# Retention by (scores · h) · w_v in place of scores · (h · w_v), with a new order of the heads' work

## The chip, the cores and the metric

The kernel runs on one core of a Trainium2 chip (trn2). The metric is the device time of one launch in microseconds (us), as the median of the runs shown. All weights come from HBM in each launch, through queues that five engines share: TensorE (PE) multiplies, ScalarE (ACT) and VectorE (DVE) prepare operands and empty PSUM, GpSimd (POOL) does a little elementwise work, SyncE (SP) issues nearly all transfers.

## What is computed

Two transformer blocks run on 256 tokens of width 1024. The part that changes is the retention of the second block. A context `ctx` of 256 tokens and the sequence `x` are normed and modulated to `hc` and `h` (1024 features each), and both give keys and values; the sequence gives queries. With the two directions and both chunk states multiplied out, what four heads (queries and keys of 256, values of 512 features) do is

```
k, v   = rows of [hc; h] @ w_k, [hc; h] @ w_v      # 512 keys; rope on the sequence's q and k
scores = (q @ k.T) / 16 * decay                    # 256 queries x 512 keys, fixed decay by distance
o      = scores @ v                                # 256 x 512 per head
on     = (o - mean) / sqrt(var + eps)              # group norm of a head's 512 values
r     += (silu(h @ w_g) * on * gn_w) @ p_ret       # summed over the heads
y      = (sigmoid(h @ w_ga) * r + sigmoid(h @ w_gf) * fourier) @ w_out
```

The sum over features of `h @ w_v` and the sum over keys of `scores @ v` can be taken in either order.

## The kernel before, in words

Every fp32 product is made of three matmuls: `mm3` (L113) multiplies high and low parts (`wh`/`hh`, `wl`/`hl`), and `split` (L104, L105) makes such a pair, the high part by a cast on ACT and the low part by a subtraction on DVE. A weight is a block of 128x1024 (512 KB): SP loads it into one of four `raw` buffers, and `split` fills one of three pairs `wh`, `wl`. So seven blocks can be ahead of TensorE. `lin` (L129) multiplies two blocks with all 256 tokens into one PSUM tile `mm`: 48 matmuls of 256 columns. `lin_tok` (L142) takes four blocks and gives a result with tokens as rows: two tiles, 48 matmuls of 512 columns. `acc_rows` (L238) adds a block's rows into four PSUM tiles that stay open (24 matmuls of 256 columns). PSUM has eight banks: two `mm`, two `at`, four `acc`.

The order on each engine is that of a scheduler which fills TensorE from whatever is ready, by the order of the program. It is fixed when the program is built, and each engine then works its list in order.

The places that the change touches, in the order of time:

- **Fourier stage.** Per group, `dft_d` and `dft_l` are two products with ACT and DVE work in between, then `four` adds into `fo`. A list `side` gives TensorE something between them: `gf` (gates, 48 matmuls), `ctx_k` (the context's keys of a head, 48) and `ctx_v` (the context's values of a head, 48 of 512 columns). Keys and values of the context go to DRAM (`kc_d`, `vc_d`), since SBUF is full.
- **Retention stage**, four heads. `ret_vg` makes the sequence's values (48 of 512 columns) and splits them into `vh`, `vl`, reads the context's values back (`vcr`) and splits them too, and makes the gate `sg` (96 of 256 columns). `ret_kq` makes key and query with rope (96 of 256) and reads the context's keys back (`kcr`). `ret_att` makes the scores `rs` (24 of 256) and multiplies them with the values into `ro` (24 of 512), then norms (`on`). `ret_rows` turns `on` (8 transposes `rt`), multiplies by gate and gain into `fz`, splits it (`zh`, `zl`), and adds four blocks of `p_ret` into `ra` (96 of 256).
- The order of heads is written by hand at the end: `ret_att(hd)`, `ret_vg(hd + 1)`, `ret_rows(hd)`, `ret_kq(hd + 1)`. In the last head the gate `sga` (eight blocks) stands where the next head's values would.

Of the kernel before, what the change touches and what calls it, by code (L numbers as in the profile page):

```python
# [11 lines left out]
FT = mybir.dt.float32  # L12
FR = mybir.dt.float32r
# [3 lines left out]
AF = mybir.ActivationFunctionType  # L17
# [8 lines left out]
PAD = 96  # L26
# [16 lines left out]
def block_kernel(ctx: ExitStack, tc: tile.TileContext, I, out):  # L43
    nc = tc.nc
    V, S, T = nc.vector, nc.scalar, nc.tensor
# [6 lines left out]
    tmp = {"gr": None, "side": 0, "first": 4, "b": 4}  # L52
# [6 lines left out]
    dram = ctx.enter_context(tc.tile_pool(name="dram", bufs=1, space=bass.MemoryType.DRAM))  # L59
# [12 lines left out]
    ident, iota, blk2 = misc[:, 0:128], misc[:, 128:256], misc[:, 256:258]  # L72
# [4 lines left out]
    def mm_tile(name="mm", tag="mm"):  # L77
        return ps.tile([128, 2, 256], FT, name=name, tag=tag)
# [35 lines left out]
    def mm3(o, lh, ll, rh, rl, start, stop, **kw):  # L114
        T.matmul(o, lh, rh, start=start, stop=False, **kw)  # L115
        T.matmul(o, lh, rl, start=False, stop=False, **kw)  # L116
        tmp["mm"] = T.matmul(o, ll, rh, start=False, stop=stop, **kw)  # L117

    def lin(srcs, rhs, sink, nk=8, eng=V):


        for j in range(0, len(srcs), 2):
            n = min(2, len(srcs) - j)
            p = mm_tile()
            for e in range(n):
# [359 lines left out]
    for n in range(2):  # L485
        p = ps.tile([128, 4, 128], FT, name="cbp", tag="mm")
# [5 lines left out]
    h = modulated(x, col("norm1_w", 0, 8), m1(1), m1(0), bc=bc1)  # L492
# [205 lines left out]
    h2 = modulated(x, col("norm2_w", 0, 8), m1(4), m1(3), gap=(mod2, 0, 3, 5))  # L698
# [125 lines left out]
    for t0 in range(0, 256, 4):  # L824
        o = wp.tile([128, 2, 4, 128], FT, name="o", tag="raw", bufs=4)
# [112 lines left out]
    V.tensor_scalar(gate, mx(2), 0.5, None, op0=OP.mult)  # L938
    cp = cst.enter_context(tc.tile_pool(name="cp", bufs=1))
    kc_d = dram.tile([4, 128, 2, 256], FT, name="kc_d")  # L940
    vc_d = dram.tile([4, 2, 128, 512], FT, name="vc_d")
    ups = ctx_ups()
    h = modulated(x, col("norm_ffn1_2", 0, 8), mx(1), mx(0), gap=(ups, 2, 12, 8))
    run(ups)
# [45 lines left out]
            nc.sync.dma_start(kc_d[hd], k)  # L990
        lin([I["w_in_2k"][2 * hd], I["w_in_2k"][2 * hd + 1]], hc, sink)

    def ctx_v(hd):
        def sink(tb, p):
            v = tmp["p"].tile([128, 512], FT, name="vcs", tag="h2")
            S.copy(v, p)
            nc.sync.dma_start(vc_d[hd, tb], v)
        lin_tok([I["w_in_2v"][hd, q] for q in range(4)], hc, sink)


    fp = cst.enter_context(tc.tile_pool(name="fp", bufs=1))
# [16 lines left out]
    def gf(j):  # L1018
        lin([I["w_in_2gf"][2 * j + i] for i in range(2)], h,
            lambda _, p: S.activation(fg[:, 2 * j:2 * j + 2], p, AF.Sigmoid))  # L1020
# [59 lines left out]
    def ret_vg(hd):  # L1080
        vh = rp2.tile([128, 4, 512], FR, name="vh", tag="vh")
        vl = rp2.tile([128, 4, 512], FR, name="vl", tag="vl")
        lin_tok([I["w_in_2v"][hd, q] for q in range(4)], h,
                lambda tb, p: split(p, vh[:, 2 + tb], vl[:, 2 + tb]))
        vcr = rp.tile([128, 2, 512], FT, name="vcr", tag="vcr")
        nc.sync.dma_start(vcr, vc_d[hd].rearrange("b p n -> p b n"))
        split(vcr, vh[:, 0:2], vl[:, 0:2])
        sg = rp2.tile([128, 4, 256], FT, name="sg", tag="sg")
        lin([I["w_in_2g"][4 * hd + i] for i in range(4)], h,
            lambda j, p: S.activation(sg[:, 2 * j:2 * j + 2], p, AF.Silu))  # L1090
        return vh, vl, sg

    def ret_kq(hd):
        kq = {}
        for nm, w in (("k", "w_in_2k"), ("q", "w_in_2q")):
            def rsink(_, p):
                ac = rp.tile([128, 2, 256], FT, name="ac", tag="ac")
                as_ = rp.tile([128, 2, 256], FT, name="as", tag="as")
                V.tensor_tensor(ac, p, cos.unsqueeze(1).to_broadcast([128, 2, 256]), op=OP.mult)
                V.tensor_tensor(as_, p, sin.unsqueeze(1).to_broadcast([128, 2, 256]), op=OP.mult)  # L1100
                r = rp.tile([128, 2, 256], FT, name="rr", tag="rr")
                V.tensor_sub(r[:, 0], ac[:, 0], as_[:, 1])
                V.tensor_add(r[:, 1], as_[:, 0], ac[:, 1])
                rh = rp.tile([128, 2, 256], FR, name=nm + "h", tag=nm + "h")
                rl = rp.tile([128, 2, 256], FR, name=nm + "l", tag=nm + "l")
                split(r, rh, rl)
                kq[nm] = (rh, rl)
            lin([I[w][2 * hd], I[w][2 * hd + 1]], h, rsink)
        kcr = rp.tile([128, 2, 256], FT, name="kcr", tag="kcr")
        nc.sync.dma_start(kcr, kc_d[hd])  # L1110
        kch = rp.tile([128, 2, 256], FR, name="kch", tag="kch")
        kcl = rp.tile([128, 2, 256], FR, name="kcl", tag="kcl")
        split(kcr, kch, kcl)
        return (kch, kcl), kq["k"], kq["q"]

    def ret_att(hd, vh, vl, kc, kx, q):
        sh = rp.tile([128, 4, 256], FR, name="sdh", tag="sdh")
        sl = rp.tile([128, 4, 256], FR, name="sdl", tag="sdl")
        for b2_, (kh, kl) in enumerate((kc, kx)):
            p = mm_tile("rs", "at")  # L1120
            for jb in range(2):
                for d in range(2):
                    m = slice(jb * 128, jb * 128 + 128)
                    mm3(p[:, jb], kh[:, d, m], kl[:, d, m], q[0][:, d], q[1][:, d], d == 0, d == 1)
            sd = rp.tile([128, 2, 256], FT, name="sd", tag="sd")
            V.scalar_tensor_tensor(sd, p, 1.0 / 16, dec[:, hd, 2 * b2_:2 * b2_ + 2], op0=OP.mult, op1=OP.mult)
            split(sd, sh[:, 2 * b2_:2 * b2_ + 2], sl[:, 2 * b2_:2 * b2_ + 2])
        on = rp.tile([128, 2, 512], FT, name="on", tag="on")
        for ib in range(2):
            t = slice(ib * 128, ib * 128 + 128)  # L1130
            p = mm_tile("ro", "at").rearrange("p a b -> p (a b)")
            for jb in range(4):
                mm3(p, sh[:, jb, t], sl[:, jb, t], vh[:, jb], vl[:, jb], jb == 0, jb == 3)
            st = rp2.tile([128, 6], FT, name="st", tag="st")
            V.bn_stats(st, p)
            mv = rp2.tile([128, 2], FT, name="mv", tag="mv")
            V.bn_aggr(mv, st)
            vv = rp2.tile([128, 1], FT, name="vv", tag="vv")
            V.tensor_scalar(vv, mv[:, 1:2], EPS, None, op0=OP.add)
            r1 = rsqrt(vv, [128, 1], "ra")  # L1140
            V.tensor_scalar(on[:, ib], p, mv[:, 0:1], r1, op0=OP.subtract, op1=OP.mult)
        return on

    def ret_rows(hd, on, sg):
# [16 lines left out]
                for e in range(2):  # L1161
                    acc_rows(acc, [rows[e]], [zs[e]], hd + c2_ + e == 0, False)

    vg, kq = ret_vg(0), ret_kq(0)
    for hd in range(4):
        on = ret_att(hd, *vg[:2], *kq)
        sg = vg[2]
        if hd < 3:
            vg = ret_vg(hd + 1)
        else:  # L1170
            lin([I["w_in_2ga"][i] for i in range(8)], h,
                lambda j, p: S.activation(sga[:, 2 * j:2 * j + 2], p, AF.Sigmoid))
# [128 lines left out]
```

## Time and profile before

| | |
|---|---|
| median of 3 runs | 2092.63 us (2092.53 to 2097.37) |
| the profiled execution: its own time | 2094.46 us |
| its span, first to last instruction | 2092.7 us |
| PE / DVE / ACT busy, share of the span | 97% / 69% / 51% |
| Fourier stage | 1460 to 1610 us of the span |
| retention stage | 1610 to 1861 us |

Matmuls are pipelined. A row of the timeline gives a matmul some 0.28 us, though the next one starts 0.113 us later, and a "busy" PE includes such overlap. What a matmul costs on TensorE is therefore taken from starts: the start of the first of a run, that of the first after it, and the count between. A gap shows as "idle before", with the releaser; it is shorter than the issue time lost, as the last matmul before it still counts as busy.

### The profile page before, as it was taken

What the parts mean: (1) busy time and instruction counts of PE and PEld (TensorE: products, weight loads), DVE (VectorE), ACT (ScalarE), POOL (GpSimd) and SP (SyncE); (2) the same over time, 40 slices, a digit from 0 to 9 for tenths busy, and PEclk for the clock granted to TensorE, in tenths of its full rate; (3) what the DMA queues carried; (4) which work ended last, traced back from release to release, by engine and by line L of the source; (5) the groups of instructions that cost most, each with busy time, mean ns of one, the idle gap of its engine ahead of it and who ended that gap; (6) DMA issues with size and microseconds to landing.
All of it is one profiled execution on the core that took longest, in us unless ns stands there. A gap on an engine that the chain in (4) does not pass through costs nothing.

```text
span 2092.7 us, 40502 instructions
## 1 busy us (share of the span) xinstructions
PE 2020.9 (97%) x16362; PEld 1932.9 (92%) x16362; DVE 1434.2 (69%) x2687; ACT 1057.8 (51%) x1754; POOL 113.9 (5%) x95
## 2 busy tenths in 40 slices
PE   6999997899999999999999999999999999999998
PEld 3987897788999999999999999999999999989998
DVE  5877989697567777777777666636644667666555
ACT  2544553598454455445555557534544444444443
POOL 1000165200000000000000000000000000010000
PEclk8999998899999999999999999999999999999998
DMA  8956644213576766767777665535456554444553
GB/s 330 332 172 233 210 162 142 80 68 134 193 244 240 250 243 242 258 240 247 244 258 254 211 218 186 202 115 163 142 191 230 183 177 151 158 137 158 194 192 111
DMA packets 115851, 413.08 MB, mean 197 GB/s; under 512 B 12880, under 2 KB 14416, under 8 KB 115152
## 3 DMA queue, kind: packets, MB, share of 16 engines
q1 hardware_dynamic: 111248, 395.29, 55.8%
q0 software_dynamic: 4128, 14.68, 2.0%
q8 instruction: 128, 2.10, 0.4%
q10 hardware_dynamic: 288, 0.52, 0.1%
q14 instruction: 59, 0.48, 0.1%
HBM read 404.15 MB, written 6.29 MB: 196 GB/s over the span
## 4 chain that ended last, share of the span: by engine, by line
PE 77%; DVE 2%; DMA 1%; issue 1%; ACT 0%; POOL 0%; DVEq 0%; SPq 0%; ACTq 0%; POOLq 0%
PE va L116 6%; PE va L117 6%; PE va L115 6%; PE ua L115 5%; PE ua L117 5%; PE ua L116 5%; PE mm L115 4%; PE mm L117 4%; PE mm L116 4%; PE fu L116 4%; PE fu L115 4%; PE fu L117 4%; PE gps L838 2%; PE fa L116 2%; PE fa L117 2%; PE fa L115 2%
## 5 line engine op out<-in xcount | busy, mean ns | idle before, releaser
L105 DVE TENSOR_TENSOR wl<-raw,wh 128x1024 fp32r<-128x1024 f32 x588 | 726.8, 1238 | 503.2 <-ACT wh L104 499.1
L104 ACT CAST wh<-raw 128x1024 fp32r<-128x1024 f32 x613 | 643.5, 1052 | 809.9 <-issue 375.7
L117 PE MATMUL ua<-hh,wl 128*128 128x256 f32 x1024 | 282.8, 276 | 1.2 <-DVE wl L105 1.2
L116 PE MATMUL va<-zl,wh 128*128 128x256 f32 x1024 | 282.3, 276 | 1.2 <-DVE zl L105 1.2
L115 PE MATMUL ua<-hh,wh 128*128 128x256 f32 x1024 | 282.8, 276 | 0.0
L115 PE MATMUL va<-zh,wh 128*128 128x256 f32 x1024 | 281.4, 276 | 1.4 <-DVE cy L464 1.4
L116 PE MATMUL ua<-hh,wh 128*128 128x256 f32 x1024 | 282.6, 276 | 0.0
L117 PE MATMUL va<-zh,wl 128*128 128x256 f32 x1024 | 282.2, 276 | 0.0
L116 PE MATMUL mm<-hh,wh 128*128 128x256 f32 x776 | 218.1, 281 | 6.1 <-DVE hh L196 6.1
L115 PE MATMUL mm<-hh,wh 128*128 128x256 f32 x776 | 217.8, 281 | 2.1 <-ACT hh L194 1.4
L117 PE MATMUL mm<-hh,wl 128*128 128x256 f32 x776 | 217.8, 281 | 0.0
L115 PE MATMUL fu<-hh,wh 128*128 128x256 f32 x704 | 195.9, 279 | 2.7 <-ACT hh L199 1.7
L116 PE MATMUL fu<-hh,wh 128*128 128x256 f32 x704 | 195.9, 278 | 0.9 <-DVE hh L200 0.9
L117 PE MATMUL fu<-hh,wl 128*128 128x256 f32 x704 | 195.6, 278 | 0.0
L116 PEld LDWEIGHTS va<-zl,wh 128*128 128x128 f32 x1024 | 192.3, 188 | 1.4 <-DVE zl L105 1.4
L117 PEld LDWEIGHTS ua<-hh,wl 128*128 128x128 f32 x1024 | 192.1, 188 | 1.6 <-DVE wl L105 1.6
L115 PEld LDWEIGHTS va<-zh,wh 128*128 128x128 f32 x1024 | 191.4, 188 | 1.6 <-DVE cy L464 1.6
L115 PEld LDWEIGHTS ua<-hh,wh 128*128 128x128 f32 x1024 | 192.4, 188 | 0.0
L117 PEld LDWEIGHTS va<-zh,wl 128*128 128x128 f32 x1024 | 192.3, 188 | 0.0
L116 PEld LDWEIGHTS ua<-hh,wh 128*128 128x128 f32 x1024 | 192.1, 188 | 0.0
L116 PEld LDWEIGHTS mm<-hh,wh 128*128 128x128 f32 x776 | 146.9, 189 | 7.3 <-DVE hh L196 6.8
L115 PEld LDWEIGHTS mm<-hh,wh 128*128 128x128 f32 x776 | 147.4, 190 | 4.5 <-ACT hh L194 1.5
(415 smaller groups left out, 4516.0 us busy)
## 6 DMA issues: line engine op xcount, KB each, us to landing
raw<-w_ffn_dram SPq DMA_DIRECT2D x176, 512.0 KB, 3.3
raw<-peer_u_dram SPq DMA_DIRECT2D x128, 512.0 KB, 4.3
raw<-peer_v_dram SPq DMA_DIRECT2D x128, 512.0 KB, 4.3
gx<-w_ada_dram SPq DMA_DIRECT2D x56, 512.0 KB, 5.5
raw<-w_ada_dram SPq DMA_DIRECT2D x40, 512.0 KB, 6.1
raw<-w_in_2v_dram SPq DMA_DIRECT2D x32, 512.0 KB, 3.9
raw<-w_in_dram SPq DMA_DIRECT2D x25, 512.0 KB, 4.4
raw<-w_out_dram SPq DMA_DIRECT2D x16, 512.0 KB, 3.2
```

What stands on the lines that cost most here:

```text
L104: S.copy(hi, src)
L105: tmp["lo"] = eng.tensor_sub(lo, src, hi.bitcast(FT))
L115: T.matmul(o, lh, rh, start=start, stop=False, **kw)
L116: T.matmul(o, lh, rl, start=False, stop=False, **kw)
L117: tmp["mm"] = T.matmul(o, ll, rh, start=False, stop=stop, **kw)
L838: mm = T.matmul(p[:, e], o[:, 0, e], o[:, 1, e], start=True, stop=True)
```

## The change

The values are not made any more. The high and low parts of `hc` and `h` are turned (128x128 transposes) so that keys are rows: `hth`, `htl`, 512 keys by 1024 features, once for all heads. `ret_h` multiplies them with the scores into `rg` (per head four PSUM tiles of 24 matmuls of 256 columns) and splits the result (`gh`, `gl`); `ret_o` multiplies that with `w_v` by `lin_tok` (48 of 512 columns), and the norm works on its result. The context's turned blocks take the way through DRAM that its values took (`hct_d`). `kcr` is read at the start of `ret_kq`. A head's rows stand behind the next head's scores and gate. The gate `sga` is made in two halves, around the last `ret_o`.

```diff
-    def ctx_v(hd):
...
+    def turned(src, c0, t, tag="mm"):
+
+        p = mm_tile("ht", tag).rearrange("p a b -> p (a b)")
+        for c in range(4):
+            T.transpose(p[:, 128 * c:128 * c + 128], src[:, c0 + c, t].bitcast(FT), ident)
+        return p
+
+    def ctx_turn(tb, part):
+        for n in range(2):
+            p = turned(hc[part], 4 * n, slice(tb * 128, tb * 128 + 128))
+            v = tmp["p"].tile([128, 512], FT, name="hts", tag="h2")
             S.copy(v, p)
-            nc.sync.dma_start(vc_d[hd, tb], v)
-        lin_tok([I["w_in_2v"][hd, q] for q in range(4)], hc, sink)
+            nc.sync.dma_start(hct_d[part, tb, :, 512 * n:512 * n + 512], v)
...
-    side = [lambda f_=f_, i=i: f_(i) for i in range(4) for f_ in (ctx_k, ctx_v)]
-    side[0:0] = [lambda j=j: gf(j) for j in range(2)]
-    side += [lambda j=j: gf(j) for j in range(2, 4)]
+    side = [lambda i=i, f_=f_: f_(i) for i in range(4) for f_ in (gf, ctx_k)]
+    for n, at in enumerate((5, 8, 10, 11)):
+        side.insert(at, lambda n=n: ctx_turn(n // 2, n % 2))
...
+    hth = rp.tile([128, 4, 1024], FR, name="hth")
+    htl = rp.tile([128, 4, 1024], FR, name="htl")
+    for part, ht in enumerate((hth, htl)):
+        nc.sync.dma_start(ht[:, 0:2].bitcast(FT), hct_d[part].rearrange("b p n -> p b n"))
+
+    def x_turn():
+        for n in range(8):
+            tb, part, c0 = n // 4, n // 2 % 2, n % 2 * 4
+            p = turned(h[part], c0, slice(tb * 128, tb * 128 + 128), "at")
...
+    def ret_h(sh, sl):
...
+        for c2_ in range(4):
+            p = mm_tile("rg", "at")
+            for e in range(2):
+                m = slice(128 * (2 * c2_ + e), 128 * (2 * c2_ + e) + 128)
+                for jb in range(4):
+                    mm3(p[:, e], hth[:, jb, m], htl[:, jb, m], sh[:, jb], sl[:, jb], jb == 0, jb == 3)
+            split(p, gh[:, 2 * c2_:2 * c2_ + 2], gl[:, 2 * c2_:2 * c2_ + 2])
+        return gh, gl
...
-        for ib in range(2):
-            t = slice(ib * 128, ib * 128 + 128)
-            p = mm_tile("ro", "at").rearrange("p a b -> p (a b)")
-            for jb in range(4):
-                mm3(p, sh[:, jb, t], sl[:, jb, t], vh[:, jb], vl[:, jb], jb == 0, jb == 3)
...
+        lin_tok([I["w_in_2v"][hd, q] for q in range(4)], g, sink)
         return on
...
+    sg, kq = None, ret_kq(0)
+    x_turn()
     for hd in range(4):
-        on = ret_att(hd, *vg[:2], *kq)
-        sg = vg[2]
-        if hd < 3:
-            vg = ret_vg(hd + 1)
-        else:
-            lin([I["w_in_2ga"][i] for i in range(8)], h,
-                lambda j, p: S.activation(sga[:, 2 * j:2 * j + 2], p, AF.Sigmoid))
-        ret_rows(hd, on, sg)
+        sd = ret_scores(hd, *kq)
+        was, sg = sg, ret_g(hd)
+        if hd:
+            ret_rows(hd - 1, on, was)
+        g = ret_h(*sd)
         if hd < 3:
             kq = ret_kq(hd + 1)
+        else:
+            ret_ga(0)
+        on = ret_o(hd, g)
+    ret_ga(2)
+    ret_rows(3, on, sg)
```

What the scheduler makes of it, at three places. First TensorE, where head 0's rows begin: before, the transposes `rt` and right behind them the first products with `zh`.

```order
L117 MATMUL mm<-hh,wl 128x256
L1150 MATMUL rt<-misc,on 128x128 x8
L115 MATMUL ra_19178<-zh,wh 128x256
L115 MATMUL ra_19179<-zh,wh 128x256
L115 MATMUL ra_19180<-zh,wh 128x256
L115 MATMUL ra_19181<-zh,wh 128x256
L116 MATMUL ra_19178<-zl,wh 128x256
```

Now 21 matmuls of the next head's `rg` stand between the two (the first four of them are shown, 17 more follow in the same way before `ra`).

```order
L117 MATMUL mm<-hh,wl 128x256
L1182 MATMUL rt<-misc,on 128x128 x8
L115 MATMUL rg<-sdh,hth 128x256
L116 MATMUL rg<-sdl,hth 128x256
L117 MATMUL rg<-sdh,htl 128x256
L115 MATMUL rg<-sdh,hth 128x256
```

Second ACT, where `rg` is emptied in the second head (`gh`), between weight casts (`wh`) and the casts of the rows (`zh`); the rows are those of the change.

```order
L104 CAST zh<-fz 128x256 x2
L104 CAST gh<-rg 128x512
L104 CAST wh<-raw 128x1024
L104 CAST zh<-fz 128x256
L104 CAST wh<-raw 128x1024
L104 CAST zh<-fz 128x256
L104 CAST wh<-raw 128x1024 x2
L104 CAST gh<-rg 128x512 x3
```

Each of the four tiles has its cast there, and no more than two weight casts stand right before one. Third the SP queue at the start of the retention stage, in the change: the reading of `hct_d` (`hth`, `htl`) and the first heads' `kcr` among the loads of weights.

```order
L82 DMA raw<-w_in_2q_dram 128x1024 x2
L1005 DMA hct_d<-hts 128x512 x2
L82 DMA raw<-w_in_2g_dram 128x1024 x2
L1091 DMA hth<-hct_d 128x2x1024
L1111 DMA kcr<-kc_d 128x512
L1005 DMA hct_d<-hts 128x512 x2
L82 DMA raw<-w_in_2g_dram 128x1024 x2
L1111 DMA kcr<-kc_d 128x512
L1091 DMA htl<-hct_d 128x2x1024
```

The loads of the first head's key and query stand ahead of all that waits here, and half of its gate's blocks too.

## Rows read from the trace of the kernel before

**Rows 1.** The page: busy time of the engines.

```profile
PE 2020.9 (97%) x16362; PEld 1932.9 (92%) x16362; DVE 1434.2 (69%) x2687; ACT 1057.8 (51%) x1754; POOL 113.9 (5%) x95
```

**Rows 2.** Busy time by stretch: length, engines (instructions), granted clock, DMA share, GB/s.

```profile
1560.00:1580.00 20.00, 20.00 (x138) 18.48 (x137) 7.53 (x7) 8.43 (x9) 0.00 (x0) 1.00 0.55 184
...
1720.00:1740.00 20.00, 18.74 (x138) 17.28 (x137) 16.31 (x45) 8.71 (x12) 0.00 (x0) 1.00 0.36 121
...
1860.00:1880.00 20.00, 17.86 (x136) 17.15 (x136) 14.13 (x22) 10.38 (x18) 6.43 (x6) 0.91 0.39 125
1880.00:1900.00 20.00, 16.14 (x121) 15.49 (x121) 14.14 (x35) 8.48 (x16) 0.00 (x0) 0.83 0.42 139
```

**Rows 3.** Who waited for whom, TensorE, 1455 to 1900: total us, times, longest.

```profile
PE ra L115 <- ACT zh L104: 3.7, 4, 0.9
...
PE ra L116 <- DVE zl L105: 1.9, 5, 0.6
PE mm L117 <- DVE wl L105: 1.5, 1, 1.5
PE mm L115 <- ACT wh L104: 1.4, 2, 0.7
```

**Rows 4.** TensorE's groups by shape, 1460 to 1862: count, busy us, mean ns.

```profile
L117 PE MATMUL mm<-wh,hc 128*128 128x512 f32 x64 | 25.1, 392 | 0.0
...
L116 PE MATMUL ro<-vl,sdh 128*128 128x512 f32 x32 | 12.6, 393 | 0.0
```

**Rows 5.** TensorE's timeline in the second head: starts of runs, between them equal matmuls.

```profile
1696.88 0.28 PE L116 MATMUL mm<-hh,wh 128*128 128x256 f32 x1
...
1705.95 0.39 PE L115 MATMUL mm<-wh,hh 128*128 128x512 f32 x1
...
1714.19 0.28 PE L115 MATMUL rs<-qh,kch 128*128 128x256 f32 x1
...
1717.06 0.39 PE L115 MATMUL mm<-wh,hh 128*128 128x512 f32 x1
...
1719.80 0.40 PE L115 MATMUL ro<-vh,sdh 128*128 128x512 f32 x1
...
1723.49 0.28 PE L115 MATMUL mm<-hh,wh 128*128 128x256 f32 x1
```

**Rows 6.** TensorE's timeline where the second head's rows begin.

```profile
1736.24 1.04 PE L1150 MATMUL rt<-misc,on 128*128 128x128 f32 x8
1738.21 0.73 PE L115 MATMUL ra<-zh,wh 128*128 128x256 f32 x4 [0.93 <-ACT zh L104]
1739.27 0.39 PE L116 MATMUL ra<-zl,wh 128*128 128x256 f32 x1 [0.33 <-DVE zl L105]
```

**Rows 7.** VectorE's timeline at the same place.

```profile
1736.87 0.88 DVE L1155 SCALAR_TENSOR_TENSOR fz<-rt,cols,sg 128x256 f32<-128x256 f32 x2 [0.61 <-PE rt L1150]
...
1738.80 0.76 DVE L105 TENSOR_TENSOR zl<-fz,zh 128x256 fp32r<-128x256 f32 x2
```

**Rows 8.** TensorE's timeline in the first head: its values, then 192 equal matmuls.

```profile
1615.16 0.39 PE L115 MATMUL mm<-wh,hh 128*128 128x512 f32 x1
...
1628.30 0.39 PE L115 MATMUL mm<-hh,wh 128*128 128x256 f32 x1 [0.71 <-DVE vl L105]
...
1651.02 0.40 PE L115 MATMUL mm<-wh,hh 128*128 128x512 f32 x1
```

**Rows 9.** The tiles of the values: ns min/median/max, first and last start, forms.

```profile
L104 ACT CAST vh<-mm x8: 587/588/590, 1626.9 to 1775.1; 128x512 fp32r<-128x512 f32 x8
L105 DVE TENSOR_TENSOR vl<-mm,vh x8: 684/688/693, 1627.5 to 1775.9; 128x512 fp32r<-128x512 f32 x8
```

**Rows 10.** The page: the splits of weights.

```profile
L105 DVE TENSOR_TENSOR wl<-raw,wh 128x1024 fp32r<-128x1024 f32 x588 | 726.8, 1238 | 503.2 <-ACT wh L104 499.1
L104 ACT CAST wh<-raw 128x1024 fp32r<-128x1024 f32 x613 | 643.5, 1052 | 809.9 <-issue 375.7
```

**Rows 11.** The tile `vcs`, the context's values on their way to DRAM.

```profile
DMA to landing us min/median/max: 3.0/3.8/5.5
```

More of the change, by code (lines that the diff above doesn't have):

```diff
@@ L940, in block_kernel @@
     kc_d = dram.tile([4, 128, 2, 256], FT, name="kc_d")
-    vc_d = dram.tile([4, 2, 128, 512], FT, name="vc_d")
+    hct_d = dram.tile([2, 2, 128, 1024], FT, name="hct_d")
     ups = ctx_ups()
@@ L991, in ctx_k @@
         lin([I["w_in_2k"][2 * hd], I["w_in_2k"][2 * hd + 1]], hc, sink)
-    def ctx_v(hd):
-        def sink(tb, p):
-            v = tmp["p"].tile([128, 512], FT, name="vcs", tag="h2")
+    def turned(src, c0, t, tag="mm"):
[7 more added lines that the diff above has]
+            v = tmp["p"].tile([128, 512], FT, name="hts", tag="h2")
             S.copy(v, p)
-            nc.sync.dma_start(vc_d[hd, tb], v)
-        lin_tok([I["w_in_2v"][hd, q] for q in range(4)], hc, sink)
+            nc.sync.dma_start(hct_d[part, tb, :, 512 * n:512 * n + 512], v)
     fp = cst.enter_context(tc.tile_pool(name="fp", bufs=1))
@@ L1078, in block_kernel, with ret_g @@
     acc = acc_tiles("ra")
[L1080 to L1087, printed above, removed]
+    hth = rp.tile([128, 4, 1024], FR, name="hth")
[6 more added lines that the diff above has]
+            p = turned(h[part], c0, slice(tb * 128, tb * 128 + 128), "at")
+            o = (hth, htl)[part][:, 2 + tb, 128 * c0:128 * c0 + 512]
+            if n % 2:
+                V.tensor_copy(o, p)
+            else:
+                S.copy(o, p)
+    def ret_g(hd):
         sg = rp2.tile([128, 4, 256], FT, name="sg", tag="sg")
@@ L1090, in ret_vg @@
             lambda j, p: S.activation(sg[:, 2 * j:2 * j + 2], p, AF.Silu))
-        return vh, vl, sg
+        return sg
     def ret_kq(hd):
+        kcr = rp.tile([128, 2, 256], FT, name="kcr", tag="kcr")
+        nc.sync.dma_start(kcr, kc_d[hd])
         kq = {}
@@ L1108, in ret_kq @@
             lin([I[w][2 * hd], I[w][2 * hd + 1]], h, rsink)
-        kcr = rp.tile([128, 2, 256], FT, name="kcr", tag="kcr")
-        nc.sync.dma_start(kcr, kc_d[hd])
         kch = rp.tile([128, 2, 256], FR, name="kch", tag="kch")
@@ L1114, in ret_kq, with ret_scores @@
         return (kch, kcl), kq["k"], kq["q"]
-    def ret_att(hd, vh, vl, kc, kx, q):
+    def ret_scores(hd, kc, kx, q):
+        rp.tile([128, PAD // 2], FT, name="pad2", tag="pad2")
         sh = rp.tile([128, 4, 256], FR, name="sdh", tag="sdh")
@@ L1124, in ret_att, with ret_o, sink @@
                     mm3(p[:, jb], kh[:, d, m], kl[:, d, m], q[0][:, d], q[1][:, d], d == 0, d == 1)
-            sd = rp.tile([128, 2, 256], FT, name="sd", tag="sd")
+            sd = rp.tile([128, 2, 256], FT, name="sd", tag="rr")
             V.scalar_tensor_tensor(sd, p, 1.0 / 16, dec[:, hd, 2 * b2_:2 * b2_ + 2], op0=OP.mult, op1=OP.mult)
             split(sd, sh[:, 2 * b2_:2 * b2_ + 2], sl[:, 2 * b2_:2 * b2_ + 2])
-        on = rp.tile([128, 2, 512], FT, name="on", tag="on")
-        for ib in range(2):
-            t = slice(ib * 128, ib * 128 + 128)
-            p = mm_tile("ro", "at").rearrange("p a b -> p (a b)")
-            for jb in range(4):
-                mm3(p, sh[:, jb, t], sl[:, jb, t], vh[:, jb], vl[:, jb], jb == 0, jb == 3)
+        return sh, sl
+    def ret_h(sh, sl):
+        rp.tile([128, 104], FT, name="pad3", tag="pad3")
+        gh = rp.tile([128, 8, 256], FR, name="gh", tag="gh")
+        gl = rp.tile([128, 8, 256], FR, name="gl", tag="gl")
+        for c2_ in range(4):
[6 more added lines that the diff above has]
+        return gh, gl
+    def ret_o(hd, g):
+        on = rp.tile([128, 2, 512], FT, name="on", tag="on")
+        def sink(ib, p):
             st = rp2.tile([128, 6], FT, name="st", tag="st")
@@ L1162, in ret_rows, with ret_ga @@
                     acc_rows(acc, [rows[e]], [zs[e]], hd + c2_ + e == 0, False)
-    vg, kq = ret_vg(0), ret_kq(0)
-    for hd in range(4):
-        on = ret_att(hd, *vg[:2], *kq)
-        sg = vg[2]
-        if hd < 3:
-            vg = ret_vg(hd + 1)
-        else:
-            lin([I["w_in_2ga"][i] for i in range(8)], h,
-                lambda j, p: S.activation(sga[:, 2 * j:2 * j + 2], p, AF.Sigmoid))
-        ret_rows(hd, on, sg)
+    def ret_ga(j):
+        lin([I["w_in_2ga"][2 * j + i] for i in range(4)], h,
+            lambda i, p: S.activation(sga[:, 2 * (j + i):2 * (j + i) + 2], p, AF.Sigmoid))
+    sg, kq = None, ret_kq(0)
+    x_turn()
+    for hd in range(4):
+        sd = ret_scores(hd, *kq)
[3 more added lines that the diff above has]
+        g = ret_h(*sd)
         if hd < 3:
             kq = ret_kq(hd + 1)
+        else:
+            ret_ga(0)
+        on = ret_o(hd, g)
+    ret_ga(2)
+    ret_rows(3, on, sg)
     mh, ml = moving("mh")
```

## The prediction

> **What bounds the kernel now.** I read the page first: TensorE is busy 97% of the span, DVE 69%, ACT 51% [rows 1]. Then the table by stretch, for the stages that change: in the Fourier stage TensorE is busy 20.00 of 20 us at the full clock while DMA has a share of 0.55, DVE 7.5 us and ACT 8.4 us; in the retention stage it still has 18.74 of 20 where a head's rows begin [rows 2]. Last the list of waits and the timeline. So these stages last as long as TensorE needs to issue their matmuls, plus a few gaps, and what DVE, ACT or DMA gains or loses counts only where it makes a gap.
>
> The price of a matmul is a distance of starts. Between 1696.88 and 1705.95 stand 80 matmuls of 256 columns: 0.1134 us each. Between 1705.95 and 1714.19 stand 36 of 512 columns: 0.229. The 24 scores after them cost 0.1196 each, the 12 further values 0.228, and 16 of `ro` 0.2306 [rows 5]. Eight transposes and the gap behind them last from 1736.24 to 1738.21; the page gives the eight 1.04 us with the tail of the last, 0.27, so a start comes every 0.11 us and the gap in issue is 1.97 - 0.87 = 1.10 us; from 1738.21 to 1739.27 four matmuls (0.45) and 0.61 us of a second gap [rows 6]. With a little after that I take 1.8 us lost per head. The list shows the same two waits in all four heads, for `zh` (3.7 us in 4) and `zl` (1.9 in 5), counted shorter because the last matmul still counts as busy [rows 3].
>
> **What the change does, part by part.**
>
> *The context's values go.* 64 matmuls on each of three lines [rows 4], 192 in all, at 0.229: -44.0 us. They stand in the Fourier stage as cover between `dft_d`, `dft_l` and `four`. Four products of 48 gate matmuls, four of 48 key matmuls and four turns of eight transposes remain for the twelve places, so each product still has 2.8 to 5.5 us of other work between it and its reader; the cast and the subtraction it waits for take 0.59 + 0.69 [rows 9], with a weight split ahead of each 3.6. I cost the lost cover at nothing; with none at all, eight products (four `dy`, four `fo`) would wait 1.3 us or more each, some 10 us.
>
> *The sequence's values become `ret_o`.* Again 192 matmuls of 512 columns, same blocks of weights, other left side: 0.
>
> *`ro` goes.* Three lines of 32 [rows 4], 96 at 0.2306: -22.1 us.
>
> *`ret_h` comes.* 4 heads x 8 feature blocks x 4 key blocks x 3 = 384 matmuls of 256 columns. No such product exists before. The nearest rows are 0.1134 for weights times `h` and 0.1196 for the scores [rows 5]: 43.5 to 45.9 us. I take +43.5, since the code puts a pad ahead of `sdh` and of `gh` as it does for `h` (`PAD`, L26), and the rows with pads are the fast ones.
>
> *Turning comes.* 32 transposes for the context and 32 for the sequence at 0.11: +7.0 us. The emptying (8 copies and 8 casts of 0.59 to 0.69 us) lies beside. The Trainium skill says more, in "TensorE: Matmul & The Clock Gate", part 4: a 128x128 transpose took about 275 ns in one kernel's context. By that the turning would be 17.6 us and the sum smaller by 10.6. The 32 transposes here are followed at 0.11 us, and 0.27 us is only the length of a single one [rows 6]; I go by the row.
>
> So far: -44.0 - 22.1 + 43.5 + 7.0 = **-15.6 us** of issue.
>
> *Gaps in the rows of heads 0 to 2.* The rows now have the next head's `rg` behind the transposes. But `rg` needs an `at` tile, and the two `at` tiles hold the turned blocks: the first is free when DVE has made two `fz` of it, at 1736.87 + 0.88 = 1737.75 [rows 7], that is 0.65 us after the last transpose was issued (1736.24 + 0.87 = 1737.11). With the way to TensorE I take 0.75 us. Then 21 matmuls (2.4 us) cover `zh` (read at 1738.21) and `zl` (done at 1739.56 [rows 7]). 1.8 becomes 0.75 in three heads: -3.2 us. The last head keeps its gaps, since only the merge follows. Ends: 0 (`fz` comes late as well) to -5.4.
>
> *The gap in head 0.* Its values waited for ACT and DVE (1.5 and 1.4 in the list [rows 3], 0.71 [rows 8]), 2.15 us in issue (its 48 matmuls last from 1615.16 to 1628.30 [rows 8], 13.14 us, against 48 x 0.229 = 11.0). The stage now begins with `ret_kq(0)`, whose blocks were loaded before. Its first `mm` tile has to be emptied of a turned block: cast of a weight 1.05 + copy 0.59 against 1.75 us of transposes, about 0.3 us. -1.8 us; ends 0 and -2.15.
>
> *The transfers.* 16 loads of 512 KB go, `vcr` becomes two larger reads: nothing, as DMA's share is 0.36 to 0.55 [rows 2]. SP holds the read of `hth` until the turned blocks have landed, 3.0 to 5.5 us after issue [rows 11], and behind it wait half a gate's weights, the next `kcr` and the second head's blocks. Four blocks stand ahead for TensorE (10.9 us of matmuls) plus two of the gate; `hth` is first read after key, query, scores and most of the gate, some 25 us on. Zero; if that cover failed, one wait of up to 10 us. `kcr`, read earlier, is waited for by ACT alone, and no wait of TensorE is put down to it [rows 3]: zero.
>
> *Norm.* `on` of a head now has 96 gate matmuls (10.9 us) between it and its transposes; before, the 86 behind `ro` were enough. Zero.
>
> **Sum:** -15.6 - 3.2 - 1.8 = **-20.6 us**. The profiled execution took 2094.46 us (span 2092.7), 1.8 above the median of the three runs. 2094.46 - 20.6 = 2073.9; on the median of 2092.63 that is **2072.0 us**, which I give. 0.3% (6.3 us) is about what a measurement of this kernel can tell from no change.
>
> **Rivals.**
>
> *A, the slow pace spreads.* From 1628.30 to 1651.02, behind two gaps, 192 of the same matmuls cost 0.1183 in place of 0.1134 [rows 8, 5], with nothing waited for. If the four heads ran so, 4 x 384 matmuls would lose 0.0049 each: +7.5, so 2079.5. For it: the change puts short gaps before each `rg`. Against: the rows of heads 1 to 3 had larger gaps, and the run of 80 after them kept 0.1134.
>
> *B, PSUM under `ret_h`.* Sixteen tiles of 24 matmuls (2.72 us) alternate in two banks, each to be emptied by 0.59 + 0.69 us [rows 9]. With one weight split ahead, 1.05 and 1.24 [rows 10], the chain is 1.05 + 1.24 + 0.69 = 2.98 or, with signals, 3.5: 0.8 us x 16 = 12.8 lost, so 2084.8. Against: for most tiles the scheduler put other matmuls between.
>
> *C, slower than before: the same place, with all three buffers' splits ahead of each tile.* ACT 3 x 1.05, then DVE's last 1.24 and 0.69: 5.08 - 2.72 = 2.36 us x 16 = 37.8 lost, so 2109.8. It decides from 1.3 us per tile on (20.6 / 16), which is two splits ahead of every tile. Against: ACT's list has at most two weight casts right before one tile in a head, and DVE is busy 69% of the span, not all of it [rows 1].
>
> *D, transposes at 0.27 us each* with no overlap, as a single one lasts [rows 6]: 64 x 0.16 = +10.4, so 2082.4. The skill's figure, above, would act like this. Against: those eight follow at 0.11.
>
> *E, the clock.* Behind the last rows the granted clock is 0.91 and 0.83 on the mean of two stretches of 20 us, in which TensorE had work for 17.86 and 16.14 us [rows 2]. That is 3.6 and 6.8 us at 1.2 GHz in place of 2.4, a loss of up to 1.8 and 3.4 us. The end of the stage comes 20 us earlier now. Either may vanish or come twice: -5 to +5. It shifts the forecast and is part of its range.
>
> **How the numbers follow.** Forecast with its bounds 0.66, A 0.12, B 0.08, D 0.06, a still larger gain (all gaps gone and fewer half-clock stretches: -20.6 - 2.3 - 5.4, about 2064) 0.04, C 0.04. The bounds of the unknown costs are +2.4 (`ret_h` at the scores' price), +3.2 and +1.8 (gaps that stay), +-5 (clock); not all at once: 2065 to 2080 around 2072. A lies inside, D just beyond; with half of D and B the range is **2064 to 2083**, leaving out about 2 in 10. Faster by over 0.3%, under 2086.3: the forecast, A, D and nearly all of B, 0.92; within 0.3%: 0.04; slower: 0.04.
>
> **What would show it.** In the profile after: 192 matmuls `mm<-wh,hc` gone, 384 `rg` at starts 0.113 apart, transposes `ht` 0.11 apart; retention stage about 20 us longer (251 us before), Fourier stage about 40 us shorter (150 before); after `rt` a gap of 0.75 us that DVE's `fz` ends. Wrong would be: `rg` at 0.118 or more (A), waits of `rg` for DVE's `gl` of 0.5 us or more a tile (B, C), `ht` at 0.27 (D), or TensorE waiting for weights behind `hth` in the queue.

## The result, and the profile after

| | us |
|---|---|
| before, median of the runs beside it | 2095.0 |
| changed kernel, median of 4 runs | 2112.15 |
| ratio, 95% interval | 1.008 (1.005 to 1.0109) |
| the same again, 12 runs: median, ratio | 2112.48, 1.0066 (1.0035 to 1.0098) |
| profiled execution read below (span) | 2107.1 (2105.3) |

The change made the kernel slower by 0.7 to 0.8%. The forecast was 2072.0, the range ended at 2083, and "slower" had a chance of 0.04: the prediction was wrong in sign. Some executions are slowed in layers that the change doesn't touch, the first profiled one of the changed kernel among them, so the ratios leave these out and the rows below come from a second profile; it stands against the 2094.46 (span 2092.7) of before, 12.6 us more.

The list of waits of TensorE from 1590 to 1875 us, the retention stage. Columns: line and tile that waited, and for what; us in all, times, the longest.

```profile
PE mm L115 <- DVE on L1172: 24.4, 4, 6.5
PE rg L115 <- DVE fz L1187: 1.9, 3, 0.6
PE ra L115 <- ACT zh L104: 0.9, 1, 0.9
PE ra L116 <- DVE zl L105: 0.9, 2, 0.6
```

The waits that the change was to shorten are shorter: `ra` for `zh` and `zl` held TensorE 5.6 us before [rows 3], now 1.8, and the `rg` that stands there waits 0.6 us a head. But on top stands a wait that the kernel before doesn't have: once in each head, `mm` waits for `on`, L1172, the last instruction of the norm. The timeline of TensorE at the first of the four (start, length, and in brackets the idle time before with what ended it):

```profile
1637.79 0.28 PE L116 MATMUL rs<-ql,kh 128*128 128x256 f32 x1
1637.91 0.28 PE L117 MATMUL rs<-qh,kl 128*128 128x256 f32 x1
1644.70 0.55 PE L115 MATMUL mm<-hh,wh 128*128 128x256 f32 x1 [6.51 <-DVE on L1172]
1645.05 0.42 PE L116 MATMUL mm<-hh,wh 128*128 128x256 f32 x1
1645.27 0.41 PE L117 MATMUL mm<-hh,wl 128*128 128x256 f32 x1
1645.48 0.41 PE L115 MATMUL mm<-hh,wh 128*128 128x256 f32 x1
...
1657.42 0.28 PE L117 MATMUL mm<-hh,wl 128*128 128x256 f32 x1
1657.54 1.04 PE L1182 MATMUL rt<-misc,on 128*128 128x128 f32 x8
1659.20 0.36 PE L115 MATMUL rg<-sdh,hth 128*128 128x256 f32 x1 [0.62 <-DVE fz L1187]
```

The output product is done at 1636.5, the scores at 1637.9, and the gate starts at 1644.70. What DVE does meanwhile:

```profile
1636.00 1.38 DVE L1166 BATCH_NORM_STATS2 st<-mm 128x6 f32<-128x512 f32 x2 [1.03 <-PE mm L117]
...
1637.38 0.66 DVE L1143 SCALAR_TENSOR_TENSOR sd<-rs,dec 128x512 f32<-128x512 f32 x1
...
1638.08 1.22 DVE L105 TENSOR_TENSOR wl<-raw,wh 128x1024 fp32r<-128x1024 f32 x1
...
1643.55 0.28 DVE L156 SCALAR_TENSOR_TENSOR ra_y<-ra_t,ra_y 128x1 f32<-128x1 f32 x2
1643.75 1.53 DVE L1172 TENSOR_SCALAR on<-mm,mv,ra_y 128x512 f32<-128x512 f32 x2
```

The norm begins with the statistics at 1636.00 and ends with the second `on` at 1645.28, 9.3 us later, and both ends read the PSUM tiles `mm`. In between come the root on 128x1 elements and other work of DVE (a weight, the scores, a key). `mm` has two buffers and `ret_o` fills both. The next product, `ret_g` of the following head (in the last head `ret_ga(2)`), also goes to `mm` and cannot start until the first of the two `on` has read its tile. Before, it was `ro` that lay under the norm, in the `at` tiles, while the next product found `mm` free. In the second head of the kernel before, the norm lasts from 1725.75 to 1735.13, 9.4 us, and TensorE goes from the last `ro` to the gate without a gap:

```profile
1726.25 0.39 PE L117 MATMUL ro<-vh,sdl 128*128 128x512 f32 x1
1726.48 0.28 PE L116 MATMUL mm<-hh,wh 128*128 128x256 f32 x1
```

```profile
1725.75 0.70 DVE L1135 BATCH_NORM_STATS2 st<-ro 128x6 f32<-128x512 f32 x1 [2.64 <-PE ro L117]
...
1734.32 0.81 DVE L1141 TENSOR_SCALAR on<-ro,mv,ra_y 128x512 f32<-128x512 f32 x1
```

The second loss stands right behind: the first gate matmuls start 0.21 us apart, later ones 0.113. The table by stretch, of the 96 gate matmuls after each wait (us, busy time of each engine, then the granted clock, DMA share, GB/s):

```profile
1644.70:1657.50 12.80, 12.80 (x96) 12.80 (x97) 4.25 (x4) 3.65 (x4) 0.00 (x0) 0.85 0.24 82
1712.70:1725.60 12.90, 12.90 (x96) 12.90 (x97) 4.25 (x4) 3.66 (x4) 0.00 (x0) 0.84 0.27 83
1780.20:1793.50 13.30, 13.29 (x96) 13.30 (x97) 4.26 (x4) 3.66 (x4) 0.00 (x0) 0.81 0.24 80
1844.60:1858.10 13.50, 13.46 (x96) 13.50 (x97) 4.29 (x4) 3.65 (x4) 0.00 (x0) 0.80 0.24 83
```

These 96 take 12.8 to 13.5 us; at the 0.1134 of [rows 5] they would take 10.9. A part of each stretch runs at 1.2 GHz, the lower of the clock's two levels. It is the clock loss that rival E saw once or twice at the end of the stage [rows 2], now in every head.

**The account.** From the first `dz` to the first `fu` of the last layer, where all the edits lie, the two profiles differ by 427.6 - 413.6 = +14.0 us:

```profile
1481.92 0.39 PE L115 MATMUL dz<-dfh,fh 128*128 128x512 f32 x1
...
1895.54 0.58 PE L115 MATMUL fu<-hh,wh 128*128 128x256 f32 x1 [1.11 <-ACT hh L199]
```

(before), and in the changed kernel:

```profile
1480.34 0.40 PE L115 MATMUL dz<-dfh,fh 128*128 128x512 f32 x1
...
1907.93 0.58 PE L115 MATMUL fu<-hh,wh 128*128 128x256 f32 x1 [1.11 <-ACT hh L199]
```

The distance from each matmul to the next, added up by tile over this stretch:

| group | before | after | difference | forecast |
|---|---|---|---|---|
| context's values, 192 | 44.1 | 0 | -44.1 | -44.0 |
| `ro`, 96 | 22.2 | 0 | -22.2 | -22.1 |
| `rg`, 384 | 0 | 44.1 | +44.1 | +43.5 |
| `ht`, 64 | 0 | 6.3 | +6.3 | +7.0 |
| `rt` and `ra` with their gaps | 55.6 | 52.7 | -2.8 | -3.2 |
| sequence's values / `ret_o`, 192, without the last head's wait | 46.3 | 44.0 | -2.3 | -1.8 |
| three waits, behind the scores | 0 | 19.4 | +19.4 | 0 |
| the fourth, behind the last `ret_o` | 0 | 5.6 | +5.6 | 0 |
| other products in `mm`, 1536 of 256 columns | 180.2 | 190.0 | +9.8 | 0 |
| the rest, the scores' own 11.5 among it | 65.4 | 65.7 | +0.3 | 0 |
| sum, before rounding | | | +14.0 | -20.6 |

All that was costed came, together to half a microsecond. 25.0 us of waits came on top, and 9.8 us in the products in `mm`: 52.6 - 4 x 10.9 = 9.0 of it is the half clock in the four stretches above, and 0.7 the distance before a turned block that waits for an emptied tile. That is the whole miss.

### The profile page after: what moved, and what is told of

The parts are those of the page before. It is cut to its first block, busy times and chain, and to the rows that moved or that the text cites. A ratio compares the mean times of both kernels' runs of the same rounds, so it can differ in the third digit from the quotient of the medians.

```text
span 2139.4 us, 40752 instructions
## 1 busy us (share of the span) xinstructions
PE 2046.7 (96%) x16522; PEld 1971.9 (92%) x16522; DVE 1417.7 (66%) x2679; ACT 1040.2 (49%) x1746; POOL 112.6 (5%) x95
## 4 chain that ended last, share of the span: by engine, by line
PE 77%; DVE 3%; DMA 1%; issue 1%; ACT 1%; POOL 0%; DVEq 0%; SPq 0%; POOLq 0%; ACTq 0%
PE va L116 6%; PE va L117 6%; PE va L115 6%; PE ua L116 5%; PE ua L117 5%; PE ua L115 5%; PE fu L116 4%; PE fu L115 4%; PE fu L117 4%; PE mm L115 4%; PE mm L116 4%; PE mm L117 4%; PE gps L838 2%; PE fa L116 2%; PE fa L117 2%; PE fa L115 2%
## 5 line engine op out<-in xcount | busy, mean ns | idle before, releaser
L105 DVE TENSOR_TENSOR wl<-raw,wh 128x1024 fp32r<-128x1024 f32 x572 | 706.9, 1237 | 542.5 <-ACT wh L104 537.0
L104 ACT CAST wh<-raw 128x1024 fp32r<-128x1024 f32 x597 | 625.4, 1050 | 848.5 <-issue 386.8
L116 PE MATMUL va<-zl,wh 128*128 128x256 f32 x1024 | 288.3, 282 | 0.9 <-DVE zl L105 0.9
L115 PE MATMUL va<-zh,wh 128*128 128x256 f32 x1024 | 286.9, 281 | 1.9 <-DVE cy L464 1.9
L117 PE MATMUL ua<-hh,wl 128*128 128x256 f32 x1024 | 287.7, 281 | 0.7 <-DVE wl L105 0.7
L117 PE MATMUL va<-zh,wl 128*128 128x256 f32 x1024 | 288.1, 282 | 0.0
L115 PE MATMUL ua<-hh,wh 128*128 128x256 f32 x1024 | 287.8, 281 | 0.0
L116 PE MATMUL ua<-hh,wh 128*128 128x256 f32 x1024 | 287.6, 281 | 0.0
L115 PE MATMUL mm<-hh,wh 128*128 128x256 f32 x776 | 223.3, 288 | 25.8 <-DVE on L1172 24.3
L116 PE MATMUL mm<-hh,wh 128*128 128x256 f32 x776 | 222.7, 287 | 6.1 <-DVE hh L196 6.1
L115 PEld LDWEIGHTS va<-zh,wh 128*128 128x128 f32 x1024 | 196.4, 192 | 2.1 <-DVE cy L464 2.1
L115 PEld LDWEIGHTS mm<-hh,wh 128*128 128x128 f32 x776 | 152.1, 196 | 28.3 <-issue 25.3
L116 PEld LDWEIGHTS mm<-hh,wh 128*128 128x128 f32 x776 | 151.9, 196 | 6.9 <-DVE hh L196 6.8
```

## The experiments

The theory: **the norm holds the PSUM tiles that the next product needs (N)**. The rival at first was a slow pace of TensorE (R), since the first profile of the changed kernel had long stretches with starts 0.118 us apart.

**The change again.** No edit.

> The changed kernel once more, on the chip of the three runs beside it, for a second profile. Theory N (the norm holds PSUM): after each head's output product TensorE stands still 5.6 to 6.8 us, because the next product of weights needs an `mm` tile and both hold the output until DVE has normed it; then it runs at half clock for 6 to 10 us. That would be four waits of some 25 us in all and four times 2.6 us for the clock, as in the first profile of the change, and a ratio to the kernel before of 1.008. A rival (R, a slow pace of TensorE: matmuls 0.118 apart in place of 0.113, as long stretches of the first profile show) would say: the loss is there, and in a profile without that pace the kernel comes out at the forecast of 2072.

Measured: 2112.48 us, ratio 1.0066, with the rows above. This profile has no long stretch of the slow pace, and is still 12.6 us over before. R is out as the cause.

**An early copy.** ACT copies the product to SBUF, the norm reads the copy:

```diff
         def sink(ib, p):
+            S.copy(on[:, ib], p)
+            p = on[:, ib]
             st = rp2.tile([128, 6], FT, name="st", tag="st")
```

> The change, but the output product is copied from PSUM to SBUF by ACT as soon as it is done, and the norm (statistics, root, scaling) reads the copy; one instruction more per half head. Theory N: `mm` comes free after a copy of 0.6 us, with at most a weight cast of 1.05 ahead, so the four waits of 5.6 to 6.8 us shrink to under 2 us each and the half clock after them goes: 27 to 36 us less than the change, 2072 to 2083, ratio to before 0.990 to 0.995. Rival R (slow pace): no difference from the change, 1.008. A second rival, H (the clock falls at these places for another reason than the wait): only the waits go, some 18 to 25 us, and the 96 gate matmuls behind the output product still take 13.4 us or more in place of 10.9.

Measured: 2079.57 us, ratio 0.993 (0.9896 to 0.9963); the stretch from `dz` to `fu` takes 400.0 us, 27.6 less than in the change. The timeline at the place of the first wait (TensorE, then ACT and DVE):

```profile
1638.14 0.28 PE L117 MATMUL rs<-qh,kl 128*128 128x256 f32 x1
1638.26 0.28 PE L115 MATMUL mm<-hh,wh 128*128 128x256 f32 x1
1638.37 0.28 PE L116 MATMUL mm<-hh,wh 128*128 128x256 f32 x1
```

```profile
1636.23 1.27 ACT L1165 COPY on<-mm 128x512 f32<-128x512 f32 x2 [2.29 <-PE mm L117]
```

```profile
1636.85 0.69 DVE L1168 BATCH_NORM_STATS2 st<-on 128x6 f32<-128x512 f32 x1 [1.66 <-ACT on L1165]
...
1648.82 0.54 DVE L1174 TENSOR_SCALAR on<-on,mv,ra_y 128x512 f32<-128x512 f32 x1
```

The norm now takes 12.5 us in place of 9.3, and the next product doesn't wait for it: the gate follows the scores at 0.12 us, and behind it the starts are 0.11 apart. So it is the buffer that counted, not the length of the chain. The 96 gate matmuls behind the scores take 10.9 us again, which puts rival H out as well. The list of waits of this kernel has a new first line, a loss that the forecast did not have:

```profile
PE rg L115 <- DVE fz L1189: 5.1, 3, 2.2
```

The norm ends later, so `fz` falls behind a weight's subtraction on DVE, and `rg`, which needs the `at` tile of the turned blocks, waits up to 2.2 us instead of 0.6.

**Filling the wait.** The scores three times over in heads 1 to 3 (the result is the same):

```diff
-            for jb in range(2):
+            for jb in [0, 1] * (3 if hd else 1):
```

> The change, with each block of the scores of heads 1 to 3 computed three times over into the same PSUM tile (48 matmuls more per head, 5.8 us of issue): TensorE has work for most of the wait of 6.2 to 6.8 us, and the wait itself, if it is for DVE's norm, ends when it ended before. Theory N: 17.3 us of matmuls are added and the time does not grow; the wait after the scores falls to about 1 us in three heads, and if the half clock comes from the standstill the 96 gate matmuls behind take 10.9 us again, three times 2.6 = 8 us less than the change: ratio to the change 0.995 to 0.998. If TensorE were the bound there: 17 us more, 1.008 of the change.

Measured: ratio 1.0042 (1.0002 to 1.0083) to before, against 1.0066 for the change. The two intervals overlap: by time, the kernel with 144 matmuls more is not slower than the change, and no more can be said. 17 us more than the change would be 1.0147 of before, which lies outside the interval. The waits from 1620 to 1880 us, then, from the table by stretch, the stretches with the first and the last of the four places:

```profile
PE mm L115 <- DVE on L1172: 5.4, 1, 5.4
PE rg L115 <- DVE fz L1187: 1.9, 3, 0.6
```

```profile
1660.00:1680.00 20.00, 20.00 (x149) 18.91 (x148) 14.36 (x40) 6.36 (x8) 0.00 (x0) 1.00 0.38 119
...
1860.00:1880.00 20.00, 14.60 (x100) 14.04 (x99) 11.12 (x35) 4.69 (x5) 0.00 (x0) 0.83 0.39 131
```

The added 17.3 us did not lengthen the stretch, so TensorE had no other work there. And the clock: at the three places without a standstill it stays at 1.00; at the fourth, where the standstill was left, it falls to 0.83. The stretch from `dz` to `fu` is 8.2 us shorter than in the change. The products in `mm` of the retention stage take 113.7 us in place of 119.8. The half clock comes from the standstill and costs some 2 us each time.

**The same hold in the kernel before.** One word there:

```diff
-            p = mm_tile("ro", "at").rearrange("p a b -> p (a b)")
+            p = mm_tile("ro", "mm").rearrange("p a b -> p (a b)")
```

> The kernel before, with one word changed: the product of scores and values, `ro`, is written to the `mm` tiles in place of the `at` tiles. Theory N: here too the next product of weights must wait until the norm has read both tiles, so the kernel before slows down by what the change lost: four waits of 5 to 7 us and up to 2.6 us of clock behind each, 20 to 36 us, ratio 1.010 to 1.017. Rival R or any cause in the new product or the turning: no difference from before, within 0.3%.

Measured: 2153.83 us, ratio 1.0265 (1.0188 to 1.0341). The forecast (1.010 to 1.017) had the sign right and the size too small; the waits from 1600 to 1920 us say why:

```profile
PE mm L115 <- DVE on L1141: 15.4, 4, 3.9
PE rs L115 <- ACT qh L104: 15.3, 4, 3.8
PE mm L115 <- DVE vl L105: 3.3, 4, 0.9
```

The first is the wait for the norm, in all four heads. The second I had not foreseen: with one pair of tiles for `ro` and the values, the values that had stood between the query and the scores came behind `ro`, and the scores wait uncovered for the query's rotation and split. So this run shows that the hold alone makes waits of this kind, but its 60 us (2153.83 against 2093.88 for the runs of before beside it) are not a measure of it.

**Two tags exchanged.** Nothing added: the output product in `at`, the scores in `mm`:

```diff
-        lin_tok([I["w_in_2v"][hd, q] for q in range(4)], g, sink)
+        lin_tok([I["w_in_2v"][hd, q] for q in range(4)], g, sink, "at")
...
-            p = mm_tile("rs", "at")
+            p = mm_tile("rs", "mm")
```

> The change with two tags exchanged and no instruction added: the output product of each head goes to the `at` tiles, where `ro` stood before, and the scores `rs` go to the `mm` tiles. The norm still reads PSUM, and takes as long as in the change. Theory N says that what counts is who needs the buffers under the norm: the 96 gate matmuls find `mm` free after one DVE instruction of 0.7 us on the scores, nothing asks for `at` until the turned blocks come, which need the norm in any case. So the four waits of 5.8 to 6.5 us and the half clock behind them go as with the early copy: 25 to 35 us less than the change, 2070 to 2080. If the long norm chain itself were the loss (rival D: DVE late, wherever its input stands), the wait would reappear at the scores or at the turned blocks and the time stay within 5 us of the change.

Measured: ratio 0.9896 (0.9849 to 0.9943), which on the 2092.63 of the first runs is 2070.9. The norm reads PSUM as in the change, no wait for `on` is left, and the stretch from `dz` to `fu` takes 402.1 us. The rival D of this run, the long chain itself, is out. From the list of waits, 1480 to 1910 us:

```profile
PE ht L997 <- ACT htl L1101: 3.0, 2, 2.3
PE rg L115 <- DVE fz L1187: 1.9, 3, 0.6
...
PE mm L115 <- DVE ra_y L151: 1.4, 3, 0.5
...
PE ht L997 <- DVE htl L1099: 0.8, 1, 0.8
```

Two small waits are new: `mm` for DVE behind the scores, 1.4 us in three heads, and `ht` for `htl`, 3.8 us in head 0, where the 24 turned blocks now follow one another without other matmuls between.

**The turned blocks in `mm` as well.** To the last run's edits:

```diff
-            p = mm_tile("rt", "at")
+            p = mm_tile("rt", "mm")
```

> As the run with the two tags exchanged, and the turned blocks `rt` of a head's rows go to the `mm` tiles too, so that the next head's `rg`, which uses `at`, does not wait until DVE has read the turned blocks. In the change that wait is 0.6 us in three heads (1.9 us in all), in the run with the early copy 5.1 us in three. Theory: it vanishes, 2 to 5 us less than the run with the two tags exchanged, 2066 to 2076. Rival: the wait only moves to the first `ra`, which needs zh and zl from the same DVE chain, and the two runs are equal within 1 us.

Measured: ratio 0.9854 (0.9804 to 0.9904), `dz` to `fu` 399.0, 3.2 less (by time the two runs' intervals overlap); `rg` waits for `fz` no more. The wait didn't move to `ra` (0.8 us); `rt` itself waits once, 1.1 us.

**Without the pads.** To the early copy:

```diff
-        rp.tile([128, PAD // 2], FT, name="pad2", tag="pad2")
...
-        rp.tile([128, 104], FT, name="pad3", tag="pad3")
```

> The run with the early copy, without the two pads that stand ahead of `sdh` and `gh`; the addresses of the operands of `ret_h` and of the output product shift, nothing else. The prediction took 0.1134 us for `rg` because the code has these pads, with the scores' 0.1196 as the other end: so `rg` should now be 0.119 to 0.120 apart, 384 x 0.006 = 2.3 us longer, and the output product up to 0.2306 in place of 0.229. If the pads did nothing, 0.1134 stays. To be read from the distances in the timeline, not from the time.

Measured, by the distances of the starts: 48 `rg` without a break take 5.74 us (0.120 each) where the change needs 5.44 (0.113), and 36 matmuls of the output product 8.42 us (0.234) against 8.24 (0.229). The order of the matmuls is that of the early copy, and the 960 other products in `mm` of the stage take 110.5 us here and 110.4 there, so a slower pace of all matmuls is not the reason. The term of 43.5 us was right because of the pads.

**A longer norm.** The root in the norm with 9 steps in place of 3:

```diff
-    def rsqrt(v, shape, name):
+    def rsqrt(v, shape, name, its=3):
...
-        for _ in range(3):
+        for _ in range(its):
...
-            r1 = rsqrt(vv, [128, 1], "ra")
+            r1 = rsqrt(vv, [128, 1], "ra", 9)
```

> The change with 9 steps of the root's iteration in place of 3 in the norm of the heads (the result of the root is the same to rounding): 18 small instructions more on DVE per half head, which run in pairs 0.195 us apart in the profile of the change, so the norm ends 6 x 3 x 0.195 = 3.5 us later in each head. Theory N: each of the four waits of TensorE grows by 3.5 us, 14 us in all, to 9.3 to 10 us, and the time by 14 us. If something else than the end of the norm released TensorE, the waits stay at 5.8 to 6.5 us.

Measured, from the list of waits:

```profile
PE mm L115 <- DVE on L1172: 38.3, 4, 10.0
```

38.3 - 24.4 = 13.9 us, where 14 was expected; `dz` to `fu` grows by 13.3. The time, 2126.93 us, is that of a single run and says no more. Each microsecond on DVE's chain is one on TensorE. The loss by the clock did not grow: the 96 gate matmuls take 12.5 to 13.7 us.

**Turning the sequence first.** To the run with three tags changed, `x_turn()` ahead of `ret_kq(0)`:

```diff
-    sg, kq = None, ret_kq(0)
-    x_turn()
+    x_turn()
+    sg, kq = None, ret_kq(0)
```

> As the run with the tags exchanged and the turned blocks in `mm`, and the turning of the sequence stands ahead of the first head's key and query in the code. In that run the 24 transposes of the sequence that follow key and query take 8.4 us with 5.6 us of waiting, for the emptying of the two `at` tiles, and the scores behind them 1.3 us more than in the other heads; now the matmuls of key and query stand between the transposes. Theory: 5 to 7 us less than that run, so a ratio to before of 0.982 to 0.983, which is 2055 to 2058 on the 2092.6 of the first runs, a stretch from the first `dz` to the first `fu` of the last layer of 392 to 394 us where before has 413.6. Rival: key and query wait instead, and nothing is gained.

Measured: ratio 0.997 (0.993 to 1.001); the rival was right, and more so: the stretch takes 402.3 us, 3.4 more than in that run. `ht` lost its waiting, and the scores got it:

```profile
PE rs L115 <- ACT qh L104: 5.3, 1, 5.3
```

The transposes had been the cover for the query's rotation and split. Behind this wait of 5.3 us the clock fell again: the 24 scores stand 0.21 us apart at a granted clock of 0.50 and take 5.6 us, where those of the early copy take 2.9.

**Early copy and turned blocks in `mm`.** To the run with the early copy:

```diff
-            p = mm_tile("rt", "at")
+            p = mm_tile("rt", "mm")
```

> As the run with the early copy, with the turned blocks in the `mm` tiles. There the first `rg` behind the turned blocks waits 5.1 us in three heads for DVE, 2.2 at most, since DVE has a weight split of 1.2 us ahead of the two reads. Theory: that wait goes, 4 to 5 us less than with the early copy: 0.990 to 0.991 of before. Rival: the wait moves to the first `ra`, equal within 1 us.

Measured: ratio 0.9905 (0.9861 to 0.9949). No wait for `on` or of `rg` for `fz` stands in its list. The stretch is 23.2 us shorter than before:

```profile
1481.85 0.40 PE L115 MATMUL dz<-dfh,fh 128*128 128x512 f32 x1
...
1872.21 0.58 PE L115 MATMUL fu<-hh,wh 128*128 128x256 f32 x1 [1.11 <-ACT hh L199]
```

9.6 us less than with the early copy alone, where 4 to 5 were expected: 7.1 lie before the last `ra`, most of it the wait that went, and 2.5 behind it, in `w_out` and the norm after it, which was not foreseen. By the stretch this is the best version found; by time it can't be told from the early copy alone or from the two with exchanged tags, whose intervals overlap with its own.

## Why the prediction was wrong

- *The context's values go, `ro` goes, `ret_h` and the turning come.* Right: -44.1 - 22.2 + 44.1 + 6.3 = -15.9 us by the table, -15.6 forecast. The lost cover in the Fourier stage cost nothing, as forecast: `dz`, `dy` and `fo` take 45.8 us where before they took 45.5. The prediction's rivals A, B and D did not come: `rg` starts 0.113 apart, with no wait for `gl`, and the transposes 0.109.
- *Gaps in the rows, gap in head 0.* Right: -2.8 and -2.3 against -3.2 and -1.8. The 0.75 us behind `rt` came as 0.79.
- *The transfers.* Right: no wait of TensorE on a load in the stage's list.
- ***Norm.*** **This step failed.** It read "`on` of a head now has 96 gate matmuls (10.9 us) between it and its transposes ... Zero." It asked who reads the norm's result, and that was indeed covered. It did not ask what the norm reads and so keeps: the 96 gate matmuls named as cover are the very ones that need the tile under the norm. `ro` lay in `at`; its successor lies in `mm`, because `lin_tok` has no other tag. The prediction noticed the same thing on a smaller scale ("`rg` needs an `at` tile, and the two `at` tiles hold the turned blocks") and did not put the question to `ret_o`. What the runs showed in place of the zero: four waits of TensorE for the norm, 25.0 us in all, which go when the norm's input is copied out or lies in `at`.
- *E, the clock.* That it could cost something was seen; the size was wrong: "-5 to +5" was drawn from two stretches at the end. Four new standstills of 5.6 to 6.7 us brought four new stretches at half clock, 9.0 us, most of the 9.8 in the table. It follows from the failed step.
- *C, slower than before*, gave 2109.8, near the result, but by another mechanism (PSUM under `ret_h`, too slow a split); its agreement is chance.
- *Two slips in its sums* change nothing: D's 64 x 0.16 is 10.2, not 10.4, and the 0.92 for "faster" leaves out the 0.04 of the still larger gain.

So -20.6 + 25.0 + 9.8 = +14.2, against +14.0 measured. Freed of the hold, the change comes out at 0.985 to 0.993 of before in four kernels, and at 0.997 in the one where the scores wait instead; the forecast was 0.990.

The list of waits of before could have warned: it has no wait for `on` at all, although the norm there is the same chain. Something had to be free for TensorE during it, and that was `mm`. The Trainium skill has the sentence for this in "Perfetto Trace Analysis", section "Optimizing Tensor Performance": independent matmul groups should rotate through different PSUM banks, so that emptying one overlaps the matmuls of the next. Here the groups do rotate, through two banks; what broke the overlap is that emptying took 9.3 us and began when both were full. The Trainium skill also says, in "Perfetto Trace Analysis", section "Optimization Strategy", that the same gap coming back on the engine that should be busy can mean too few buffers for the next tile; the four waits of 5.4 to 6.5 us agree.

## What to carry to other kernels

When a product moves to another helper, ask of its PSUM tile who reads it last and which product asks for that tag next; a chain of small instructions that reads PSUM at both ends holds the tile for its whole length, however little of it is work on the tile. Copy such a tile out at once, or put it under a tag that nobody needs meanwhile; both came to about the forecast gain here (0.993 and 0.990 of before). And count a standstill of TensorE of some 6 us with what comes behind it: here about 2 us at half clock each.

## What the runs showed of the hardware

**A slow pace at full clock.** In the kernel before, 192 gate matmuls stand 0.1183 us apart from 1628 to 1651 us, and 80 of the same shape 0.1134 from 1697 to 1706 [rows 8, 5], with the granted clock at 1.00 in both. In one profile of the changed kernel the starts are 0.118 us apart from about 515 to 1225 us, in another 0.113 there, with the same instructions. A stretch of the one, then the same of the other (the counts are matmuls and weight loads in 20 us):

```profile
800.00:820.00 20.00, 20.00 (x172) 20.00 (x171) 15.27 (x23) 9.73 (x15) 0.00 (x0) 1.00 0.67 237
```

```profile
800.00:820.00 20.00, 20.00 (x179) 20.00 (x179) 14.28 (x20) 10.65 (x16) 0.00 (x0) 1.00 0.70 240
```

172 against 179 matmuls is 4%, and over 710 us some 28 us. No wait stands there. What starts and ends it was not tried, and stays open.

**The distance of matmuls depends on where the operands lie.** Removing two small pads moved `rg` from 0.113 to 0.120 us and the 512-column product from 0.229 to 0.234, with the same instructions in the same order.

**The clock's loss hardly depends on the length of the standstill.** Waits of 5.4 to 6.5 us and of 9 to 10 us were followed by about the same loss, 1.6 to 2.8 us in 96 matmuls. A shorter stop can do it too, but need not: with the early copy `rg` waited 2.2 us in two heads, behind the same matmuls, and the granted clock of the next 3 us was 0.55 in one and 1.00 in the other. What decided between them was not tried.
